# A hand-written order of the tensor engine's side work: joining lone transposes to other small work in the first attention

## The chip, the cores and the metric

One core of one Trainium2 chip runs the whole kernel. The metric is the time of one execution on the device, in microseconds (us). The engines are PE (TensorE, matrix products and transposes, with PEld for its weight loads), ACT (ScalarE), DVE (VectorE), POOL (GpSimd) and SP (SyncE, which issues most DMAs). Each works through a queue of its own in order; they wait for each other on semaphores.

## The reference

A trunk of two layers on `x` of 512 tokens by 1024. The change lies in layer 0, a differential attention with six heads, in parallel with a four-head cross-attention into 256 memory tokens:

```
proj = rms_norm(x) @ w_in_diff            # q, k, v of 6 heads, and the memory's queries
q, k = rms_norm(q) * d**-0.5, rms_norm(k) # per head and map, d = 64, two maps a head
logits = q @ k.T + bias                   # blocks of 128 queries, only the keys of past blocks
p = softmax(logits)                       # per map
w = p[map 0] - lam * p[map 1]
o = rms_norm(w @ v)
x = x + concat(o, memory attention) @ w_out
x = x + conv_ffn(rms_norm(x))
```

Layer 1 has a gated linear attention in place of the differential one; it and the two feed-forward parts are not touched.

## The kernel before, in words

The large products are computed in three terms from operands split into a high and a low part (`whi`, `wlo` for weights, `xsh`, `xsl` for activations), lines 328 to 330 in `gemm`. Weights come by DMA into `raw`, ACT casts them to `whi` (L251) and DVE subtracts for `wlo` (L254). The products of the first attention (`qk` of head pairs 1 and 2, values, the memory's keys and values, the memory's queries) lie in a queue `F` of small pieces, each with an estimated cost, in `ORDER`.

Around these products PE has small work to do for heads whose inputs are ready. Its order is written out by hand in `SCRIPT`: a number lets `F` put out products of about so many microseconds, a letter with a number is one step. PE's instructions stand exactly in that order; those of ACT and DVE are put in order by the framework, which starts from the same program order and may move a later instruction ahead. The steps that matter here:

- `P h`, `prepare`: turns (transposes) the normed `qs` and `ks` of head `h`, four 128x128 blocks each, into a PSUM bank, and ACT copies them to `qT` and `kT` (L696). Heads 2p and 2p+1 share the `qs`, `ks` of pair p.
- `L t`, `M t`, `logits`: the logits of step t (L733) into two banks, `lg` or `tp`; then DVE adds the bias and takes the maximum (L740), ACT takes the exponential (L743), and DVE joins the two maps (L748, L749, L752). There are 15 such steps, five for each pair.
- `T t`, `turn`: transposes the weights of step t into a `tp` bank; ACT copies them to `xt` (L762).
- `V t`, `values`: multiplies them by the values (L774) into an `sm` bank; where a head is complete, `output` follows (Squares, L785). `s h` scales it, `F h` (`finish`) turns it and splits it into high and low (L308, L309).
- `N i`, `norms`: `group_norm` of `qs` or `ks` of a pair, with no work for PE: Squares on ACT (L384), sums on DVE (L385), the reciprocal root on both (L232 to L240), and the multiplication in place on DVE (L390). N4 and N5 are `qs` and `ks` of pair 2, which `P4` and `P5` turn.
- `a`, `b`: operands from the memory tokens. `token_rsqrt` transposes sums of squares of the tokens and makes their reciprocal roots `r_mem`, by which the memory's products are scaled as they leave PSUM.

PSUM has eight banks, two for each of the tags `mm`, `sm`, `lg` and `tp`; a step that asks for a bank waits until the reader of the one before has done.

Of the kernel before, what the change touches and what calls it, by code (L numbers as in the profile page):

```python
# [36 lines left out]
VNAMES = ('v0', 'v0', 'v2')  # L37

SCRIPT = """
    17.75 P0 3.9  # L40
    L0 M1 a3 3.4 P1 5.05 a0 0.97
    1.94 a1 T0
    L2 M3 a2 3.57
    T1 4.86 N2 V0 T2 N3 V1 12.33
    L4 P2 4.55 P3 1.62 V2 T3 2.27 T4
    L5 M6 s0 V3 b1 2.6 V4 1.3 T5 1.3
    L7 M8 3.5 T6 F0 3.64 b0
    V5 T7 8.42 V6 s1 N5 N4 F1
    L9 V7 P4 b2 4.45 T8 T9 s2 3.0
    L10 V8 3.55 X P5 q0  # L50
    L11 b3 V9 T10 4.2
    L12 F2 V10 s3 T11 3.8 q1 k0
# [126 lines left out]
def trunk(ctx, tc, head_d, x_t, mem_t, wpack, cols_a_d, cols_d, conv_d, gate_d, rel_bias, diff_lambda, consts, onehot, out):  # L179
# [12 lines left out]
    def bank(tag):  # L192
        return ps.tile([128, 512], F32, name=f"ps_{tag}", tag=tag)

    def xtile():
        return xs.tile([128, S], F32, name="xt", tag="xs", bufs=XS)

    def split_tiles(pool=None, tag="xs", bufs=XS):
        pool = pool or xs
        return (pool.tile([128, S], F32R, name=tag + "h", tag=tag, bufs=bufs),  # L200
                pool.tile([128, S], F32R, name=tag + "l", tag=tag, bufs=bufs))

    def small(name, bufs=None):
        return cp.tile([128, 16], F32, name=name, tag=name, bufs=bufs)

    def blk(b, w=128):
        return slice(w * b, w * b + w)
# [8 lines left out]
    def transpose(dst, src):  # L216
        n = src.shape[0]
        nc.tensor.transpose(dst, src, ident[:n, :n])  # L218
# [10 lines left out]
    def rsqrt(src, n, inv, on_dve=False, y=None, later=False):  # L229
        v, t = small("rs_v")[:, :n], small("rs_t")[:, :n]  # L230
        y = small("rs_y")[:, :n] if y is None else y
        V.tensor_scalar(v, src, inv, EPS, op0=ALU.mult, op1=ALU.add)  # L232
        if on_dve:
            V.tensor_scalar(t.bitcast(I32), v.bitcast(I32), 1, None, op0=ALU.logical_shift_right)
            V.tensor_scalar(y.bitcast(I32), t.bitcast(I32), -1.0, 1597463007.0, op0=ALU.mult, op1=ALU.add)
            newton(v, y, t)
            newton(v, y, t)
        else:
            A.activation(y, src, AF.Ln, scale=inv, bias=eps)
            A.activation(y, y, AF.Exp, scale=-0.5)  # L240
        if later:
            return y, lambda: newton(v, y, t)
        newton(v, y, t)
        return y
# [48 lines left out]
    def weights(key, by_block=False):  # L293
        i = used[0]
        assert plan[i][0] == key, (plan[i][0], key)
        limit = first_of[i] + WB if by_block else first_of[min(i + 2, len(plan))]
        while done[0] < min(max(limit, first_of[i + 1]), len(order)):
            make_block()
        used[0] += 1
        parts, made[i] = made[i], None  # L300
        return parts

    def freed(i, k):
        if k in [sum(len(b[2]) for b in blocks[i][:j + 1]) - 1 for j in range(len(blocks[i]))] and done[0] < len(order):
            make_block()

    def split(hi, lo, src, gain):
        A.activation(hi, src, AF.Copy, scale=gain)  # L308
        V.scalar_tensor_tensor(lo, src, gain, hi.bitcast(F32), op0=ALU.mult, op1=ALU.subtract)  # L309
# [5 lines left out]
    def gemm(sh, sl, nb, key, w, evac, hook=None, late=False, spare=False):  # L315
        got, open_ = [], {}

        piece = [q[0] for q in plan].index(key)

        def unit(b, k0, k1):  # L320
            if not got:
                got.extend(weights(key, True))
            if k0 == 0:
                open_[b] = bank("tp" if spare and b == 0 else "lg" if late and b > 1 else "mm")[:, :w]
            p = open_[b]
            for k in range(k0, k1):
                hi, lo = got[k]
                mm(p, sh[k][:, blk(b)], hi, start=k == 0, stop=False)  # L328
                mm(p, sh[k][:, blk(b)], lo, start=False, stop=False)  # L329
                mm(p, sl[k][:, blk(b)], hi, start=False, stop=k == KT - 1)  # L330
                if b == nb - 1:
                    freed(piece, k)
            if k1 == KT:
                if hook is not None and b == 0:
                    hook()
                evac(b, open_.pop(b))
        units = [(b, k) for b in range(nb) for k in range(0, KT, 2)]
        if late:
            units.sort(key=lambda u: u[0] == nb - 1 or u[1] == KT - 2)
        for b, k in units:  # L340
            F.add(6 * w / 2370.0, lambda b=b, k=k: unit(b, k, k + 2))
# [23 lines left out]
    r_mem = perm.tile([128, 2], F32, name="r_mem")  # L365

    def col(i, t=cols):
        return t[:, i:i + 1]
# [4 lines left out]
    c_dq, c_dk = col(16), col(17)  # L373
# [52 lines left out]
    def token_rsqrt(tag, sq, nb, y, on_dve=False):  # L426
        p, ss = bank(tag), small("ss")[:, :nb]
        for b in range(nb):
            transpose(p[:, blk(b)], sq[:, blk(b)])
        V.reduce_sum(ss, p[:, :128 * nb].rearrange("p (b n) -> p b n", b=nb), axis=AX.X)  # L430
        return rsqrt(ss, nb, 1.0 / D, on_dve, y=y)
# [11 lines left out]
    with tc.tile_pool(name="ini", bufs=1) as ip, tc.manual_schedule(engines={E.Activation, E.DVE, E.Pool, E.SP}):  # L443
# [8 lines left out]
        p = bank("tp")  # L452
# [48 lines left out]
        for k in range(KT):  # L501
# [24 lines left out]
            for b, i, t in todo:  # L526
                xp, w = terms[i]
# [11 lines left out]
    mem_acc = [None]  # L539

    def mem_squares():
        for i in range(4):
            squares(memT[i], mem_acc)
        sq = mem_acc[0]
        V.tensor_add(sq[:, 0:256], sq[:, 0:256], sq[:, 256:512])


    def mem_kv(l):
        hs, ls = [None] * KT, [None] * KT
        km = [None]  # L550

        def operands(ks=range(KT)):
            if l == 0 and km[0] is None:
                mem_squares()
            if km[0] is None:
                km[0] = xtile().rearrange("p (b n) -> p b n", b=2)
            for k in ks:
                if k % 2 == 0:
                    mh, ml = split_tiles()
                c = blk(k % 2, 256)  # L560
                hs[k], ls[k] = mh[:, c], ml[:, c]
                split(hs[k], ls[k], memT[k // 2][:, c], c_mem(l, k))

        def ev(b, p):
            A.activation(km[0][:, b], p[:, :256], AF.Copy, scale=r_mem[:, b:b + 1])
            A.activation(vm[l][:, b], p[:, 256:], AF.Copy, scale=r_mem[:, b:b + 1])

        def keys(tag="lg"):
            F.need(f"kv{l}")
            p = bank(tag)  # L570
            for hp in range(2):
                for b in range(2):
                    transpose(p[:, 256 * hp + 128 * b:256 * hp + 128 * b + 128], km[0][:, b, blk(hp)])
            A.activation(kmT[l].rearrange("p a b -> p (a b)"), p, AF.Copy, scale=c_mk(l))
        gemm(hs, ls, 2, ("kv", l), 512, ev,
             (lambda: token_rsqrt("lg", mem_acc[0], 2, r_mem)) if l == 0 else None)
        F.add(0.0, lambda: group_norm(None, km[0], 2, 4, 64))
        F.mark(f"kv{l}")
        return operands, keys
# [79 lines left out]
    def diff_layer(pool, mix, acc):  # L659
# [8 lines left out]
        qk = {}  # L668

        def halves(d0, d1):  # L670
            def ev(b, p):
                A.activation(d0[:, b], p[:, :256], AF.Copy, scale=r[:, b:b + 1])
                A.activation(d1[:, b], p[:, 256:], AF.Copy, scale=r[:, b:b + 1])
            return ev
# [13 lines left out]
        def prepare(h):  # L688
            pr, j = divmod(h, 2)
            t2 = []  # L690
            for src, g, nm in zip(qk[pr], (c_dq, c_dk), ("qT", "kT")):
                dst = pool.tile([128, S], F32, name=nm, bufs=3)
                p = bank("tp")
                for b in range(NB):
                    transpose(p[:, blk(b)], src[:, b, blk(j)])
                A.activation(dst, p, AF.Copy, scale=g)  # L696
                t2.append(dst)
            if j == 0:
                pairs[pr] = dict(s2=small("smd").rearrange("p (m b) -> p m b", b=8), nm=small("nmd"), rc=small("rcd"))
            heads[h] = dict(q=t2[0], k=t2[1], v=vs[pr], j=j, left=NB)  # L700
# [106 lines left out]
        ev = halves(*qk[0])  # L807
# [4 lines left out]
        ma = MemAttn(pool, 0, qm, mix, False)  # L812
        ops, keys = [None] * 2, [None] * 2
        for key in ORDER:
# [19 lines left out]
            "N": lambda i: norms(i // 2, i % 2), "a": lambda i: ops[0]((2 * i, 2 * i + 1)),  # L834
            "b": lambda i: ops[1]((2 * i, 2 * i + 1)), "k": lambda i: keys[i]("sm"),
            "q": lambda i: ma.queries() if i else (F.need("v2"), ma.norm()),
            "l": lambda i: ma.logits(i), "t": ma.turn, "v": lambda i: ma.values(i, "sm"),
            "s": lambda i: scales.pop(i)(), "X": lambda i: load_x(x_t),
            "O": lambda i: last.append(out_proj(0, mix, 1, acc, 5)), "!": lambda i: F.flush()}
        do(SCRIPT, doing)  # L840
# [226 lines left out]
    def load_x(src):  # L1067
        for k in range(KT):
            xT[k] = xtile()
            nc.sync.dma_start(xT[k], src[k])  # L1070
# [208 lines left out]
```

## Time and profile before

| what | us |
|---|---|
| median of 3 runs | 1164.59 (1164.59 to 1164.97) |
| the profiled execution, its own time | 1164.66 |
| its span, first to last instruction | 1162.9 |
| PE busy | 1158.3 |
| DVE busy | 752.8 |
| ACT busy | 544.9 |

How to read the lines below. A row of a timeline has the start in us from the span's start, the time to the end of the last of the grouped instructions, the engine, the line of the kernel, the operation, output<-inputs, shapes, and how many; in brackets the idle time of the engine before it and what ended that. Matmuls overlap: one starts before the one ahead has ended, so their cost is read from start to start. A row of the view of waits has who waited, for whom, us in total, how many times, and the longest. `ps_tp` is a bank of tag `tp`, and so on; `C` holds the identity by which PE transposes.

### The profile page before, as it was taken

The numbers are of one execution on the slowest core, as the hardware profiler recorded it, in microseconds if no ns is written. First come the engines' busy times: TensorE is split into PE (matmuls) and PEld (weight loads), VectorE is DVE, ScalarE is ACT, GpSimd is POOL, SyncE is SP. The second block draws the span as 40 slices with busy tenths as digits, with TensorE's granted clock in tenths as the row PEclk, the third lists the DMA queues.
The fourth block names the chain that finished last, engine by engine and source line by source line (L and its number), as shares of the span: only waits on it lengthen the run. The fifth ranks groups of instructions, "written<-read, shape, count | busy, mean of one in ns | idle before, by whom it ended". The sixth has DMA issues, their size and how long they took to land.

```text
span 1162.9 us, 14782 instructions
## 1 busy us (share of the span) xinstructions
PE 1158.3 (100%) x5648; PEld 965.8 (83%) x5648; DVE 752.8 (65%) x1261; ACT 544.9 (47%) x951; POOL 6.5 (1%) x30
## 2 busy tenths in 40 slices
PE   9999999999999999999999999999999999999998
PEld 7888887888888888888888888988888888888887
DVE  7676778688677326677457637867976733576741
ACT  6677686555344213344337634436544421344420
POOL 0000000000000000000000000000000000000000
PEclk9999999999999999999999999999999999999999
DMA  8522242233223223222342220332332323232231
GB/s 285 175 82 83 78 144 70 73 108 128 73 93 125 87 82 121 73 99 94 121 145 68 93 98 11 121 110 101 107 111 73 108 92 109 90 110 73 91 100 45
DMA packets 39652, 117.70 MB, mean 101 GB/s; under 512 B 4767, under 2 KB 7256, under 8 KB 39582
## 3 DMA queue, kind: packets, MB, share of 16 engines
q1 hardware_dynamic: 39150, 116.37, 29.5%
q8 instruction: 44, 0.72, 0.3%
q10 hardware_dynamic: 432, 0.39, 0.1%
q14 instruction: 26, 0.21, 0.1%
HBM read 112.54 MB, written 4.21 MB: 100 GB/s over the span
## 4 chain that ended last, share of the span: by engine, by line
PE 99%; DMA 0%; ACT 0%; DVE 0%; DVEq 0%; issue 0%
PE ps_mm L349 9%; PE ps_mm L350 9%; PE ps_mm L351 9%; PE ps_sm L351 8%; PE ps_sm L349 8%; PE ps_sm L350 8%; PE ps_mm L328 6%; PE ps_mm L330 6%; PE ps_mm L329 6%; PE ps_lg L349 3%; PE ps_tp L351 3%; PE ps_tp L349 3%; PE ps_lg L351 3%; PE ps_lg L350 3%; PE ps_tp L350 3%; PE ps_tp L218 3%
## 5 line engine op out<-in xcount | busy, mean ns | idle before, releaser
L251 ACT CAST whi<-raw 128x1024 fp32r<-128x1024 f32 (+4 forms) x212 | 207.8, 986 | 255.9 <-PE ps_tp L350 120.9
L254 DVE TENSOR_TENSOR wlo<-raw,whi 128x1024 fp32r<-128x1024 f32 (+4 forms) x212 | 240.5, 1139 | 116.3 <-ACT whi L251 115.5
L349 PE MATMUL ps_mm<-xsh,whi 128*128 128x512 f32 x438 | 171.6, 392 | 0.0
L350 PE MATMUL ps_mm<-xsl,whi 128*128 128x512 f32 x438 | 170.6, 389 | 0.0
L351 PE MATMUL ps_mm<-xsh,wlo 128*128 128x512 f32 x438 | 170.5, 389 | 0.0
L349 PE MATMUL ps_sm<-xsh,whi 128*128 128x512 f32 x378 | 147.0, 389 | 0.0
L350 PE MATMUL ps_sm<-xsl,whi 128*128 128x512 f32 x378 | 147.0, 389 | 0.0
L351 PE MATMUL ps_sm<-xsh,wlo 128*128 128x512 f32 x378 | 147.0, 389 | 0.0
L328 PE MATMUL ps_mm<-whi,xsh 128*128 128x512 f32 (+2 forms) x328 | 126.6, 386 | 0.0
L1127 ACT ACTIVATE cvo<-u,cv 128x512 f32<-128x512 f32 x88 | 71.4, 815 | 112.1 <-DVE u L1125 112.1
L330 PE MATMUL ps_mm<-whi,xsl 128*128 128x512 f32 (+2 forms) x328 | 123.0, 375 | 0.0
L329 PE MATMUL ps_mm<-wlo,xsh 128*128 128x512 f32 (+2 forms) x328 | 122.8, 374 | 0.0
L351 PEld LDWEIGHTS ps_mm<-xsh,wlo 128*128 128x128 f32 x438 | 82.2, 188 | 17.2
L350 PEld LDWEIGHTS ps_mm<-xsl,whi 128*128 128x128 f32 x438 | 82.3, 188 | 17.1 <-DVE xsl L309 0.4
L349 PEld LDWEIGHTS ps_mm<-xsh,whi 128*128 128x128 f32 x438 | 82.2, 188 | 17.0 <-issue 0.3
L1128 DVE SCALAR_TENSOR_TENSOR cvo<-u,cv,cvo 128x512 f32<-128x512 f32 x88 | 65.7, 748 | 36.2 <-ACT cvo L1127 36.0
L350 PEld LDWEIGHTS ps_sm<-xsl,whi 128*128 128x128 f32 x378 | 70.9, 188 | 14.7
L351 PEld LDWEIGHTS ps_sm<-xsh,wlo 128*128 128x128 f32 x378 | 70.9, 188 | 14.7
L349 PEld LDWEIGHTS ps_sm<-xsh,whi 128*128 128x128 f32 x378 | 70.9, 188 | 14.7
L330 PEld LDWEIGHTS ps_mm<-whi,xsl 128*128 128x128 f32 x328 | 61.7, 188 | 11.4
L328 PEld LDWEIGHTS ps_mm<-whi,xsh 128*128 128x128 f32 x328 | 61.7, 188 | 11.1 <-issue 0.7
L329 PEld LDWEIGHTS ps_mm<-wlo,xsh 128*128 128x128 f32 x328 | 61.8, 188 | 10.0
(309 smaller groups left out, 1777.7 us busy)
## 6 DMA issues: line engine op xcount, KB each, us to landing
raw<-in_wpack_dram SPq DMA_DIRECT2D x178, 512.0 KB, 3.4
xt<-in_x_t_dram SPq DMA_DIRECT2D x15, 256.0 KB, 5.6
raw<-in_wpack_dram SPq DMA_DIRECT2D x15, 256.0 KB, 5.5
raw<-in_wpack_dram SPq DMA_DIRECT2D x8, 384.0 KB, 3.6
xres<-xt SPq DMA_DIRECT2D x8, 256.0 KB, 3.0
xt<-xres SPq DMA_DIRECT2D x8, 256.0 KB, 5.2
out_dram<-xt SPq DMA_DIRECT2D x7, 256.0 KB, 2.0
bt<-bias_d SPq DMA_DIRECT2D x6, 256.0 KB, 4.7
```

Of the source, the lines that this page charges most:

```text
L218: nc.tensor.transpose(dst, src, ident[:n, :n])
L251: ins = A.copy(hi[:, c], raw[:, c])
L254: V.tensor_sub(lo[:, c], raw[:, c], hi[:, c].bitcast(F32))
L328: mm(p, sh[k][:, blk(b)], hi, start=k == 0, stop=False)
L329: mm(p, sh[k][:, blk(b)], lo, start=False, stop=False)
L330: mm(p, sl[k][:, blk(b)], hi, start=False, stop=k == KT - 1)
L349: mm(p, hi[:, blk(n)], bh, start=i == first, stop=False)
L350: mm(p, hi[:, blk(n)], bl, start=False, stop=False)
L351: mm(p, lo[:, blk(n)], bh, start=False, stop=i == last)
L1127: A.activation(c, u[:, 2:], AF.Identity, scale=cv[l][:, 2, j:j + 1], bias=cv[l][:, 3, j:j + 1])
L1128: V.scalar_tensor_tensor(c, u[:, 1:S + 1], cv[l][:, 1, j:j + 1], c, op0=ALU.mult, op1=ALU.add)
```

## The change

In the script, turns that stood between two runs of products are moved next to other small steps: P1 directly behind P0; T1 behind V0, and V1 behind T2; P3 ahead of L4, with P2 behind it; T5 behind V4; T6 and F0 directly ahead of V5, T7; T8 ahead of V6; T9 ahead of L10. The numbers around them are joined, so that about the same products come out between the steps. P1 turns into the two `sm` banks in place of `tp`. The two transposes of the memory tokens' sums, which hung as a hook on a piece of the memory's products, become a step `w` behind V1. The number of instructions for PE stays the same; what is computed does not change. Two lines fewer stand in the kernel, so its later lines have numbers smaller by one or two.

```diff
 SCRIPT = """
-    17.75 P0 3.9
-    L0 M1 a3 3.4 P1 5.05 a0 0.97
+    17.75 P0 P1 3.9
+    L0 M1 a3 8.45 a0 0.97
     1.94 a1 T0
-    L2 M3 a2 3.57
-    T1 4.86 N2 V0 T2 N3 V1 12.33
-    L4 P2 4.55 P3 1.62 V2 T3 2.27 T4
-    L5 M6 s0 V3 b1 2.6 V4 1.3 T5 1.3
-    L7 M8 3.5 T6 F0 3.64 b0
-    V5 T7 8.42 V6 s1 N5 N4 F1
-    L9 V7 P4 b2 4.45 T8 T9 s2 3.0
+    L2 M3 a2 8.43 N2 V0 T1 N3 2.6 T2 V1 w 9.73
+    P3 L4 P2 6.17 V2 T3 2.27 T4
+    L5 M6 s0 V3 b1 2.6 V4 T5 2.6
+    L7 M8 7.14 T6 F0 b0
+    V5 T7 8.42 T8 V6 s1 N5 N4 F1
+    L9 V7 P4 b2 4.45 s2 3.0 T9
     L10 V8 3.55 X P5 q0
...
-        gemm(hs, ls, 2, ("kv", l), 512, ev,
-             (lambda: token_rsqrt("lg", mem_acc[0], 2, r_mem)) if l == 0 else None)
+        gemm(hs, ls, 2, ("kv", l), 512, ev)
...
-            for src, g, nm in zip(qk[pr], (c_dq, c_dk), ("qT", "kT")):
+            for src, g, nm, tag in zip(qk[pr], (c_dq, c_dk), ("qT", "kT"), {1: ('sm', 'sm')}.get(h, ("tp", "tp"))):
                 dst = pool.tile([128, S], F32, name=nm, bufs=3)
-                p = bank("tp")
+                p = bank(tag)
...
+            "w": lambda i: token_rsqrt("lg", mem_acc[0], 2, r_mem),
```

More of the change, by code (lines that the diff above doesn't have):

```diff
@@ L836, in diff_layer @@
             "q": lambda i: ma.queries() if i else (F.need("v2"), ma.norm()),
-            "l": lambda i: ma.logits(i), "t": ma.turn, "v": lambda i: ma.values(i, "sm"),
+            "w": lambda i: token_rsqrt("lg", mem_acc[0], 2, r_mem), "l": lambda i: ma.logits(i), "t": ma.turn, "v": lambda i: ma.values(i, "sm"),
             "s": lambda i: scales.pop(i)(), "X": lambda i: load_x(x_t),
```

## The prediction

> **What bounds the kernel now.** First the page: engines, chain, clock.
>
> ```profile
> span 1162.9 us, 14782 instructions
> PE 1158.3 (100%) x5648; PEld 965.8 (83%) x5648; DVE 752.8 (65%) x1261; ACT 544.9 (47%) x951; POOL 6.5 (1%) x30
> PEclk9999999999999999999999999999999999999999
> PE 99%; DMA 0%; ACT 0%; DVE 0%; DVEq 0%; issue 0%
> ```
>
> TensorE (PE) is busy all the span and makes 99% of the chain that ended last. Then the view of waits, for PE alone, in whole:
>
> ```profile
> PE ps_tp L454 <- PEq L1234: 0.8, 1, 0.8
> PE ps_mm L528 <- ACT xsh L308: 0.2, 1, 0.2
> ```
>
> After 5 us PE waits for nobody. So there are two ways to move the end: fewer nanoseconds of PE work, or a wait that PE does not have now. A new wait goes into the end in full, since no idle time stands behind it to swallow it. ACT and DVE have room on average, but they run their queues in order: what matters is where a short instruction stands in them, not how busy they are.
>
> **What the change moves.** The built programs hold the same 5333 PE instructions, and SP's and POOL's stand in the same order, so no DMA (weights, bias) moves past another one. PE's order changes inside the first attention only, and ACT's and DVE's with it. I call a run of turns, values and logits between two runs of products an island. Between 47 and 160 us six islands go: P1 joins P0, the two turns of the memory norm join V1 (step w), T1 joins V0, P3 joins L4 P2, T5 joins V4, and T6 F0 join V5 T7 while T8 goes ahead of V6 and T9 ahead of L10.
>
> **Term 1: six islands fewer, a gain.** The timeline of PE around T7 (42 products follow it, to 140.00):
>
> ```profile
> 130.22 0.60 PE L218 MATMUL ps_tp<-C,xt 128*128 128x128 f32 x4
> 130.57 0.48 PE L328 MATMUL ps_mm<-whi,xsh 128*128 128x512 f32 x1
> 130.89 0.40 PE L329 MATMUL ps_mm<-wlo,xsh 128*128 128x512 f32 x1
> 131.12 0.40 PE L330 MATMUL ps_mm<-whi,xsl 128*128 128x512 f32 x1
> ...
> 138.41 0.39 PE L329 MATMUL ps_mm<-wlo,xsh 128*128 128x512 f32 x1
> ...
> 140.00 0.39 PE L330 MATMUL ps_mm<-whi,xsl 128*128 128x512 f32 x1
> 140.23 1.05 PE L774 MATMUL ps_sm<-vv,xt 128*128 128x128 f32 x8
> 141.12 0.60 PE L218 MATMUL ps_tp<-C,o 128*128 128x128 f32 x4
> 141.65 1.13 PE L733 MATMUL ps_lg<-kT,qT 64*128 64x256 f32 x8
> 142.71 1.16 PE L774 MATMUL ps_sm<-vv,xt 128*128 128x128 f32 x8
> 143.71 0.60 PE L218 MATMUL ps_tp<-C,qs 128*128 128x128 f32 x4
> 144.14 0.60 PE L218 MATMUL ps_tp<-C,ks 128*128 128x128 f32 x4
> ```
>
> Starts tell the cost, since the durations overlap. A settled product takes (140.00 - 138.41) / 7 = 0.227. After the turn at 130.22 the next product starts 0.35 later, and the 41 steps from 130.57 to 140.00 take 9.43 instead of 41 x 0.227 = 9.31. A turn that stands alone therefore costs 0.35 + 0.12 = 0.47; one with another turn behind it costs 143.71 to 144.14 = 0.43. Joining an island saves 0.04 to 0.05 and no more: 6 x 0.05 = 0.3. Ends: nothing (a turn's own work is the same anywhere) and twice as much, 0.6.
>
> **Term 2: T8 ahead of V6 holds up the norms of pair 2, a loss.** P4's first four transposes (143.71) need `qs` of pair 2 after its norm, steps N5 N4: Squares on ACT (L384), sums and reciprocal roots, and a multiplication on DVE (L390). The timelines of ACT and DVE show when that is done now:
>
> ```profile
> 130.34 0.47 ACT L673 ACTIVATE ks<-ps_mm,r_x 128x256 f32<-128x256 f32 x1
> ...
> 131.50 0.58 ACT L762 COPY xt<-ps_tp 128x512 f32<-128x512 f32 x1
> 131.96 1.17 ACT L384 ACTIVATE xt<-ks 128x512 f32<-128x512 f32 x2
> ...
> 141.75 0.69 ACT L308 ACTIVATE xsh<-ps_tp,cols 128x512 fp32r<-128x512 f32 x1 [1.85 <-PE ps_tp L218]
> ```
>
> ```profile
> 134.51 0.68 DVE L385 TENSOR_REDUCE ss<-xt 128x8 f32<-128x512 f32 x1
> ...
> 135.93 1.23 DVE L390 TENSOR_TENSOR ks<-ks,rs_y 128x1024 f32<-128x1024 f32 x1
> ...
> 137.49 1.23 DVE L390 TENSOR_TENSOR qs<-qs,rs_y 128x1024 f32<-128x1024 f32 x1
> 142.48 0.75 DVE L309 SCALAR_TENSOR_TENSOR xsl<-ps_tp,cols,xsh 128x512 fp32r<-128x512 f32 x1 [3.77 <-ACT xsh L308]
> 143.14 0.68 DVE L740 CUSTOM_DVE_ANT_0 xt<-ps_lg,bt 128x512 f32<-128x512 f32 x1
> ...
> 143.75 0.69 DVE L740 CUSTOM_DVE_ANT_0 xt<-ps_lg,bt 128x512 f32<-128x512 f32 x1
> ```
>
> The four Squares start at 131.96, right behind T7's copy (L762), and the multiplied `qs` is there at 137.49 + 1.23 = 138.72: a chain of 6.76, done 5.0 before P4. In the changed build the script has T8 ahead of N5 N4, and ACT's queue has T8's copy directly ahead of the four Squares (before, T8 came after P4):
>
> ```
> L760 TensorCopy xt_1506<-ps_tp_1501      (T8's copy)
> L383 Activation xt_1519<-ks_459 ... xt_1539<-qs_458   (the four Squares)
> ```
>
> So the Squares can't start before PE has turned T8, behind the 42 products. In the times of before (earlier terms shift everything alike):
>
> - T8 starts where V6 stands, 140.23, and is turned at 140.23 + 0.60 = 140.83. F1's rows (141.12 + 0.60, ACT at 141.75) give 0.03 until ACT starts, so the copy is at 140.86, and the Squares 131.96 - 131.50 = 0.46 later, at 141.32. That is 9.4 later than now.
> - The chain of 6.76 ends at 148.08 if nothing else stands in its queues. But it now runs when F1 and L9 do, and in the built order DVE has F1's low half (142.48 to 143.14, 0.66) and L9's two bias sums (0.61 each, 143.14 to 143.75) ahead of the `qs` multiplication: 1.88 together. Part of it falls into the hole of the chain where DVE waits for ACT's Ln and Exp, 134.51 + 0.68 = 135.19 to 135.93, 0.74. At least 1.88 - 0.74 = 1.1 is added; at most 1.88 and F1's 0.69 on ACT, which stands between a Ln and its Exp, 2.6. I take 1.4, near the lower end, because the low half is about as long as the hole. `qs` is ready at 149.5.
> - PE asks for it at 143.71 plus T8's 0.43 = 144.14.
>
> The wait is 149.48 - 144.14 = 5.3, with ends 5.1 and 6.5. Queued behind it on PE are P4, the rest of the products and thus everything; all of it moves. Nothing is late next: during the wait ACT, DVE and the weights' DMAs run ahead.
>
> A stall of that length may cost more than itself. The timeline of PE at the start:
>
> ```profile
> 0.77 3.32 PE L454 MATMUL ps_tp<-const-float32-0.0 128*128 128x512 f32 x6 [0.77 <-PEq L1234]
> 4.29 1.33 PE L528 MATMUL ps_mm<-whi,xsh 128*128 128x256 f32 x4 [0.20 <-ACT xsh L308]
> 5.43 1.05 PE L528 MATMUL ps_sm<-whi,xsh 128*128 128x512 f32 x2
> 6.28 0.66 PE L528 MATMUL ps_mm<-wlo,xsh 128*128 128x512 f32 x2
> 6.77 0.62 PE L528 MATMUL ps_sm<-wlo,xsh 128*128 128x512 f32 x2
> 7.23 0.62 PE L528 MATMUL ps_mm<-whi,xsl 128*128 128x512 f32 x2
> ```
>
> Two products take 0.85 at 5.43 and 0.46 from 6.77: PE runs at about half speed until 6.3, 5.5 after its first matmul, though the page's PEclk shows full tenths there. No row shows what an idle PE does later, since it never is. [...] In the sum I leave it at nothing and make it a rival, priced from the rows.
>
> **Term 3: banks asked for sooner, a small loss.** The turning banks (`tp`) are two. Where islands merge, a turn asks for a bank that ACT has not yet emptied. Rows of ACT:
>
> ```profile
> 31.75 0.52 ACT L673 ACTIVATE ks<-ps_sm,r_x 128x256 f32<-128x256 f32 x1
> ...
> 94.19 1.05 ACT L251 CAST whi<-raw 128x1024 fp32r<-128x1024 f32 x1 [0.52 <-DMA raw<-in_wpack_dram]
> 95.48 0.21 ACT L240 ACTIVATE rs_y<-rs_y 128x8 f32<-128x8 f32 x1
> 98.14 0.67 ACT L696 ACTIVATE qT<-ps_tp,cols 128x512 f32<-128x512 f32 x1
> 126.10 1.99 ACT L251 CAST whi<-raw 128x1024 fp32r<-128x1024 f32 x2
> ```
>
> P3 L4 P2: P2 asks about 2.0 after P3 starts (two turns of 0.43, logits of 1.06 as 141.65 to 142.71). P3's first copy can start when ACT is through its weights and roots (95.69) and takes 0.67: free at about 96.4, asked for at 94.9 + 2.0. It fits, unless the weights' cast, which waits for a DMA, is 0.5 later: then 0.3 for each bank. T6 F0 V5 T7: T7 asks for T6's bank 1.75 after T6 (0.43, 0.43, 0.89); ACT has a cast of 1.0, two evacuations and the copy of 0.58 to do in that time: 0 to 0.5. I take 0.2 at each place, 0.4 together, ends 0 and 1.1.
>
> P1's early turns take the `sm` banks, emptied by 31.75 + 0.52, long before P0 and P1: nothing. Covers: its two copies on ACT delay a weight cast by 1.3, hidden by two pieces of weights in hand; without that, up to 1.3. Step w makes the memory's roots in another place, still ahead of the first evacuation that scales by them: nothing.
>
> **Sum.** The profiled execution took 1164.66 (span 1162.9, and 1.8 around it), 0.07 over the median of 1164.59. 5.3 + 0.4 - 0.3 = +5.4: 1170.1 us. Own range 1169.2 (5.1 + 0 - 0.6) to 1172.3 (6.5 + 1.1).
>
> **Rivals.**
>
> - *The clock falls in the stall.* PE comes back at half speed. Price from the start: a slow stretch of 2.0 (4.29 to 6.28) to 5.5 us, of which 0.47 is lost (0.43 against 0.23 for a product), 0.9 to 2.6; middle 1.7. Time: 1171.8. For it: the slow start. [...]
> - *The stall is not there: not slower.* If the four Squares ran ahead of T8's copy, as ACT has them before, the chain ends at 138.7, 5 us ahead of P4, and what is left is +0.4 - 0.3: 1164.7. It turns on one place, whether L384 on `ks` starts before T8 is turned. `ks` itself is evacuated by 130.34 + 0.47 = 130.81, so data allows it; the order of ACT's queue speaks against it.
> - *The change does not do what it says.* Turns side by side cost 0.43 and alone 0.47: with no gain at all the sum is 0.3 higher, 1170.4, within the range. Alone it decides nothing.
>
> **How the numbers follow.** Forecast 0.53, clock 0.43, no stall 0.03, the rest 0.01. The range takes the forecast's own low end rounded, 1169.0, and up to 1173.0, which holds the clock's middle with the upper half of its price; outside lie the early Squares and the longest slow stretches. A measurement of this kernel can tell 0.2%, 2.3 us: slower than 1166.9 are the forecast and the clock, 0.96; within 0.2% 0.03; faster 0.01.
>
> **What would show it.** In the profile after: a wait of 5 to 6 us of PE for DVE `qs` at P4, near 144 to 150 us, the first entry of PE's waits; the Squares on `ks` at about 141, behind T8's copy; no other wait of PE over 0.5. PE's busy time, the wait left out, falls by 0.3. If the clock fell, products behind P4 start 0.43 apart for some us. Wrong would be: Squares at 132, a wait under 3 us, or a PE time that grows elsewhere.

## The result and the profile after

| kernel | median us | lowest to highest | ratio to before, 95% interval |
|---|---|---|---|
| before | 1164.59 | 1163.94 to 1164.97 (5 runs) | |
| after | 1172.66 | 1171.74 to 1175.09 (5 runs) | 1.0072 [1.0061, 1.0084] |

The changed kernel is 0.7% slower, 8.1 us. The forecast was 1170.1, its range ended at 1173.0. The median lies inside, 2.6 above the forecast, one of the five runs (1175.09) lies outside, and the case that happened is the rival in which the clock falls.

The profiled execution of after took 1172.66 itself. From its page, the same lines that were shown of before, with the row of slices of the granted clock:

```profile
span 1170.9 us, 14783 instructions
PE 1160.8 (99%) x5648; PEld 967.6 (83%) x5648; DVE 751.6 (64%) x1261; ACT 545.7 (47%) x951; POOL 6.5 (1%) x30
PEclk9999989999999999999999999999999999999999
PE 95%; ACT 2%; DVE 1%; DMA 1%; issue 0%; DVEq 0%; ACTq 0%
```

The span grew by 8.0. PE's busy time grew by 2.5, although it has the same 5648 instructions, and where the prediction had a fall of 0.3: something ran slower. The chain that ended last now goes through ACT and DVE for 3% of the span, and in the sixth slice, 146 to 176 us, the digit of the clock is an 8. The view of waits, PE alone, in whole:

```profile
PE ps_tp L217 <- DVE rcd L746: 5.2, 1, 5.2
PE ps_tp L453 <- PEq L1232: 0.8, 1, 0.8
PE ps_tp L217 <- ACT qT L694: 0.2, 1, 0.2
```

There is one new wait of 5.2 us (the 0.2 for `qT` is P2's, at 96.60). The view names the DVE instruction that it takes for the releaser, a small one right behind; what P4's transposes read is `qs`, whose multiplication (L389) ends at nearly the same moment, 149.36 against 149.43. The timelines of PE, ACT and DVE of after, around the place:

```profile
139.94 0.40 PE L329 MATMUL ps_mm<-whi,xsl 128*128 128x512 f32 x1
140.17 0.60 PE L217 MATMUL ps_tp<-C,xt 128*128 128x128 f32 x4
...
149.51 1.08 PE L217 MATMUL ps_tp<-C,qs 128*128 128x128 f32 x4 [5.25 <-DVE rcd L746]
...
151.67 0.63 PE L328 MATMUL ps_mm<-wlo,xsh 128*128 128x512 f32 x1
152.10 0.63 PE L329 MATMUL ps_mm<-whi,xsl 128*128 128x512 f32 x1
...
155.08 0.40 PE L327 MATMUL ps_mm<-whi,xsh 128*128 128x512 f32 x1
155.32 0.40 PE L328 MATMUL ps_mm<-wlo,xsh 128*128 128x512 f32 x1
```

```profile
140.81 0.59 ACT L760 COPY xt<-ps_tp 128x512 f32<-128x512 f32 x1 [0.96 <-PE ps_tp L217]
141.30 1.15 ACT L383 ACTIVATE xt<-ks 128x512 f32<-128x512 f32 x2
```

```profile
147.33 0.68 DVE L738 CUSTOM_DVE_ANT_0 xt<-ps_lg,bt 128x512 f32<-128x512 f32 x1
148.14 1.22 DVE L389 TENSOR_TENSOR qs<-qs,rs_y 128x1024 f32<-128x1024 f32 x1
```

Read in this order: T8's turn (140.17), its copy on ACT (140.81), the Squares behind it (141.30), one of L9's bias sums on DVE, ahead of the multiplication (147.33), the multiplied `qs` (148.14 + 1.22 = 149.36), P4 (149.51). Behind P4 the products start 0.43 apart (151.67 to 152.10), and only from 155.08 on 0.24. The view of stretches shows the granted clock there; its columns are the stretch, its length, PE's busy time and instructions, the granted clock, and the DMAs' share and rate:

```profile
148.20:148.24 0.04, 0.00 (x0) 1.00 0.00 0
148.26:148.30 0.04, 0.00 (x0) 0.50 0.00 0
155.08:155.12 0.04, 0.04 (x2) 1.00 0.00 0
148.25:151.66 3.41, 2.15 (x9) 0.50 0.23 77
151.66:155.07 3.41, 3.41 (x9) 0.50 0.00 0
```

The clock was halved at 148.25, while PE waited, and came back by 155.08: 6.83 us, in 2.15 + 3.41 = 5.56 of which PE had work. In the 3.41 us ahead of the fall, 144.84 to 148.25, PE did nothing at all.

The profile shows one execution. Half speed for 6.83 us makes a mean granted clock of 1 - 0.5 x 6.83 / 1171 = 0.997. Four of the five executions of after have this mean on record; the fifth, 1171.74, has 0.999, so it spent at most about 3.5 us at half speed. The length of the slow stretch is not the same every time.

**Where the 8 us came from**, by starts on PE. P0 starts at 46.72 here, at 47.11 in before; the last product starts at 1166.88 here, at 1158.88 in before:

```profile
46.72 0.60 PE L217 MATMUL ps_tp<-C,qs 128*128 128x128 f32 x4
...
1166.88 0.39 PE L350 MATMUL ps_tp<-midh,wlo 128*128 128x512 f32 x1
```

```profile
47.11 0.60 PE L218 MATMUL ps_tp<-C,qs 128*128 128x128 f32 x4
...
1158.88 0.39 PE L351 MATMUL ps_tp<-midh,wlo 128*128 128x512 f32 x1
```

- P0 to the last product ahead of T8: 139.94 - 46.72 = 93.22, where before had 140.00 - 47.11 = 92.89: the joins cost 0.33.
- The wait: 5.25.
- P4 to the end: 1166.88 - 149.51 = 1017.37. Before had 1158.88 - 143.71 = 1015.17 with T8's turn of 0.43 inside, so 1014.74: 2.63 more, by the clock.
- Sum 8.21. P0 itself came 0.39 sooner in this execution; the remainder to the 8.00 at the last product, 0.18, lies between T8 and P4. Nearly all of it comes from the way the wait is counted: idle time begins at the end of the values, 143.10 + 1.16, while P4 would have started 1.00 after their start (142.71 to 143.71 in before), 0.16 sooner. By starts the wait is 5.41.

### The profile page after: what moved, and what is told of

Its sections match the earlier page's. It is cut to its first block, busy times and chain, and to the rows that moved or that the text cites. A ratio compares the mean times of both kernels' runs of the same rounds, so it can differ in the third digit from the quotient of the medians.

```text
span 1170.9 us, 14783 instructions
## 1 busy us (share of the span) xinstructions
PE 1160.8 (99%) x5648; PEld 967.6 (83%) x5648; DVE 751.6 (64%) x1261; ACT 545.7 (47%) x951; POOL 6.5 (1%) x30
## 4 chain that ended last, share of the span: by engine, by line
PE 95%; ACT 2%; DVE 1%; DMA 1%; issue 0%; DVEq 0%; ACTq 0%
PE ps_mm L348 9%; PE ps_mm L350 9%; PE ps_mm L349 9%; PE ps_sm L348 7%; PE ps_sm L350 7%; PE ps_sm L349 7%; PE ps_mm L327 5%; PE ps_mm L329 5%; PE ps_mm L328 5%; PE ps_tp L350 3%; PE ps_lg L350 3%; PE ps_tp L348 3%; PE ps_lg L348 3%; PE ps_lg L349 3%; PE ps_tp L349 3%; PE ps_tp L217 3%
```

## The experiments

The lines changed are those of the script; after has `V5 T7 8.42 T8 V6 s1 N5 N4 F1` and, below it, `L9 V7 P4 b2 4.45 s2 3.0 T9`.

**1. T8 and T9 back, all other moves kept** (after as the base):

```diff
-    V5 T7 8.42 T8 V6 s1 N5 N4 F1
-    L9 V7 P4 b2 4.45 s2 3.0 T9
+    V5 T7 8.42 V6 s1 N5 N4 F1
+    L9 V7 P4 b2 4.45 T8 T9 s2 3.0
```

> The changed kernel with T8 back behind P4, next to T9, as it was before; the five other joins stay. Theory (T8's copy holds up the norms of pair 2, and the clock falls in the wait that follows): the wait of 5.2 us at P4 and the slow stretch both go, the clock stays 1.000, and what is left are the other joins: 1164.4 us, 0.2 less than before, at most 0.5 apart from it. Rival (the joins themselves, the memory's roots in step w, or banks asked for sooner cost the time): the time stays near 1172.

Measured: 1164.69 (1164.26 to 1165.88), ratio 1.0003 [0.9995, 1.0012], granted clock 1.000. Its view of waits has no entry for P4, and its timeline of PE around the joins is:

```profile
46.60 0.60 PE L217 MATMUL ps_tp<-C,qs 128*128 128x128 f32 x4
...
139.80 0.39 PE L329 MATMUL ps_mm<-whi,xsl 128*128 128x512 f32 x1
```

139.80 - 46.60 = 93.20, again 0.31 more than before. The whole loss beyond that goes with T8.

**2. T8 alone moved, nothing else** (before as the base):

```diff
-    V5 T7 8.42 V6 s1 N5 N4 F1
-    L9 V7 P4 b2 4.45 T8 T9 s2 3.0
+    V5 T7 8.42 T8 V6 s1 N5 N4 F1
+    L9 V7 P4 b2 4.45 T9 s2 3.0
```

> The kernel before with one edit alone: T8 ahead of V6, T9 where it was. Theory: the whole loss is here, a wait of 5.2 to 5.4 us of TensorE at P4 on the norm of qs, and a fall of the clock that costs up to 2.6 us more: 1170 to 1173 us, as in the changed kernel. Rival (the joins share the loss): well under 1170.

Measured: 1171.96 (1171.46 to 1173.03), 1.0068 [1.0055, 1.0081]. P4 in its timeline of PE:

```profile
149.90 1.09 PE L218 MATMUL ps_tp<-C,qs 128*128 128x128 f32 x4 [5.25 <-DVE rcd L748]
```

One step moved makes the wait and the slow clock (slow from 148.56 to 155.39, 6.83 again). The two experiments together show that T8's place is sufficient and, in this kernel, necessary.

**3. T8 stays ahead of V6, the norms go ahead of the products** (after as the base). This tells the queue of ACT from the place of T8 as such:

```diff
-    V5 T7 8.42 T8 V6 s1 N5 N4 F1
+    V5 T7 N5 N4 8.42 T8 V6 s1 F1
```

> The changed kernel with T8 still ahead of V6, but with N5 N4 ahead of the products that come before T8, so that the Squares stand in front of T8's copy in ScalarE's queue. Theory (the order of copy and Squares in the queue): Squares at about 132 us, no wait at P4, clock 1.000, 1164.3 us. Rival (T8's place on TensorE, or what VectorE does for F1 and L9 at that time, holds P4 up): a wait of 1 to 5 us at P4 stays.

Measured: 1165.07 (1164.48 to 1167.21), 1.001 [1.0002, 1.0019]. ACT has the Squares behind T7's copy, as in before, and P4 does not wait (the only entry of 0.2 in its view of waits is P2's, at 99.04):

```profile
133.74 0.58 ACT L760 COPY xt<-ps_tp 128x512 f32<-128x512 f32 x1
134.21 1.17 ACT L383 ACTIVATE xt<-ks 128x512 f32<-128x512 f32 x2
```

T8 can stay where the change put it; what costs is that the Squares stand behind a copy that comes so late. The 0.8 over the expectation is mostly the joins, counted at -0.3 there and measured at +0.3 (49.15 to 142.33 on PE, 93.18). The profiled execution was the longest one, 1167.21: its first products ran at half speed until about 10 us, which is told at the end.

**4 and 5. PE kept busy in the wait.** A step `D` between V7 and P4 runs 22 products that nobody reads, into an `lg` bank (4) or a `tp` bank (5):

```diff
-    L9 V7 P4 b2 4.45 s2 3.0 T9
+    L9 V7 D P4 b2 4.45 s2 3.0 T9
...
+        def keep_busy():
+            p = bank("lg")      # kept_busy_tp: bank("tp")
+            for i in range(22):
+                mm(p, xh[i % KT][:, blk(0)], xh[(i + 1) % KT], start=True, stop=True)
...
```

> The changed kernel with 22 more products (128x512, some 5.0 us) that nobody reads between V7 and P4: they fill the wait and do no work of the result. Theory (the 2.6 us beyond the wait come from the clock, which falls because TensorE idles): the wait shrinks to 0.2 to 0.6 us, the clock stays 1.000, products behind P4 start 0.23 apart, and the time is 1169.6 to 1170.2 us, 2.5 under the changed kernel. Rival (TensorE is slow behind the wait because weights, copies or banks have to start again): products behind P4 start later than 0.23 apart as before, and the time stays near 1172.6.

Measured: 1171.88 (1171.57 to 1172.07), 1.0065 [1.0051, 1.0079]; the expectation was missed by 1.7. The timeline of PE shows that the filler spoilt the experiment:

```profile
146.28 5.30 PE L833 MATMUL ps_lg<-xsh 128*128 128x512 f32 x22 [1.98 <-DVE nmd L738]
151.42 0.60 PE L217 MATMUL ps_tp<-C,qs 128*128 128x128 f32 x4
```

It waited 1.98 for DVE to read L9's logits out of the bank, and P4 came at 151.42, 1.9 later than in after. 1170.1 + 1.9 is what was measured. So it was run again with the other bank:

> As kept_busy, but the 22 products that nobody reads go into a tp bank, which is empty by then, in place of a lg bank, which VectorE still read for L9: there the filler itself waited 2.0 us and left TensorE 1.9 us later than needed. Theory (the 2.6 us beyond the wait come from the clock, which falls because TensorE idles): filler from 144.1 to 149.1, a wait of 0.2 to 0.6 us at P4, clock 1.000, products behind P4 0.23 apart, 1169.8 to 1170.4 us. Rival (starting again behind a wait costs it): near 1172.6 us.

Measured: 1170.7 (1169.82 to 1172.32), 1.0049 [1.0037, 1.0062]. The median is 0.3 over what the clock theory expected, and 2.0 under after. The profiled execution took 1169.82, its granted clock was 1.000, and PE goes straight through:

```profile
143.72 5.27 PE L833 MATMUL ps_tp<-xsh 128*128 128x512 f32 x22
149.22 0.63 PE L217 MATMUL ps_tp<-C,qs 128*128 128x128 f32 x4 [0.23 <-DVE rcd L746]
...
150.35 0.39 PE L328 MATMUL ps_mm<-wlo,xsh 128*128 128x512 f32 x1
150.58 0.40 PE L329 MATMUL ps_mm<-whi,xsl 128*128 128x512 f32 x1
...
1163.91 0.39 PE L350 MATMUL ps_tp<-midh,wlo 128*128 128x512 f32 x1
```

From P4 to the last product, the same instructions as in after: 1163.91 - 149.22 = 1014.69, against 1017.37. With P4 at nearly the same moment, the slow clock alone is worth 2.68 in these two executions; the medians differ by 2.0.

**6. A shorter wait.** 2.12 us of products moved behind T8:

```diff
-    V5 T7 8.42 T8 V6 s1 N5 N4 F1
+    V5 T7 6.3 T8 2.12 V6 s1 N5 N4 F1
```

> The changed kernel with T8 2.1 us of products sooner, in an island of its own ahead of V6: T8's copy, the Squares and the end of the norm come 2.1 us sooner, and TensorE asks for qs when it did. Theory: a wait of 3.1 to 3.4 us at P4. [...] If the wait did not come from T8's copy, it stays 5.2 us and the time near 1172.

Measured: 1170.32 (1169.84 to 1171.37), 1.0043 [1.003, 1.0057]. The wait shrank to 3.27, so 1164.7 + 3.3 = 1168.0 is what it would give with a full clock. The profiled execution took 1171.37, and its timeline of PE and its stretches show the clock falling all the same:

```profile
148.10 1.09 PE L217 MATMUL ps_tp<-C,qs 128*128 128x128 f32 x4 [3.27 <-DVE rcd L746]
```

```profile
146.72:146.76 0.04, 0.00 (x0) 0.50 0.00 0
153.56:153.60 0.04, 0.04 (x1) 1.00 0.00 0
143.29:146.70 3.41, 1.54 (x14) 1.00 0.01 2
```

It fell at 146.70, when PE had stood still for 146.70 - (148.10 - 3.27) = 1.87 us: in the 3.41 us before, PE was busy for 1.54, 45%. It was back 6.8 us later, by 153.56. From P4 to the last product it took 1165.60 - 148.10 = 1017.50, 2.8 more than in kept_busy_tp. The other four runs, 1.8 to 2.4 above 1168.0, have no trace. Their mean granted clock is 0.998 in one and 0.999 in three, against 0.997 in the profiled one, so they spent less time at half speed. No run without a wait has 0.998. Some have 0.999, as the profiled execution of keep_gains below, whose clock is 0.50 only behind the last product, from 1161.2 on; so in those three a shorter fall is likely, not shown.

**7. Are the joins worth anything?** After with P3, T6 F0, T8 and T9 where before has them, the other joins kept:

```diff
-    P3 L4 P2 6.17 V2 T3 2.27 T4
+    L4 P2 4.55 P3 1.62 V2 T3 2.27 T4
...
-    L7 M8 7.14 T6 F0 b0
-    V5 T7 8.42 T8 V6 s1 N5 N4 F1
-    L9 V7 P4 b2 4.45 s2 3.0 T9
+    L7 M8 3.5 T6 F0 3.64 b0
+    V5 T7 8.42 V6 s1 N5 N4 F1
+    L9 V7 P4 b2 4.45 T8 T9 s2 3.0
```

> The changed kernel with those joins undone that brought a wait: P3, T6 with F0, and T8 with T9 stand as before; P1 with P0, T1 with V0, step w and T5 with V4 stay. Four islands fewer than before, no new wait. From the first small turns to the last product the trace should be 0.1 to 0.2 us shorter than that of the kernel before, by the saving seen up to 93 us in the changed kernel (0.12); the time 1164.3 us, which the runs can't tell from before. If joins cost more than they save, it is longer than before by 0.1 or more.

Measured: 1164.49 (1164.21 to 1164.99), 0.9995 [0.9986, 1.0004]. The timeline of PE:

```profile
46.86 0.60 PE L217 MATMUL ps_tp<-C,qs 128*128 128x128 f32 x4
...
139.62 0.39 PE L329 MATMUL ps_mm<-whi,xsl 128*128 128x512 f32 x1
```

92.76 against 92.89: 0.13. In this stretch the trace has 13 islands where before has 16 (and after 11): three fewer, not the four that were expected, since T1 in joining V0 splits T2 and V1 off. That is 0.04 each, seen in the starts of one execution and too small for the times. It is the best version found, and not measurably better than before.

**8 and 9. How long may PE wait?** Experiment 5 with fewer products in the filler:

```diff
-            for i in range(22):
+            for i in range(16):     # filler_11: range(11)
```

> As kept_busy_tp with 16 in place of 22 products that nobody reads: TensorE works until about 147.7 us and then waits some 1.6 us at P4 for the norm, which is ready at the same time as before. [...]

> The same with 11 such products: a wait of some 2.7 us at P4. [...]

Waits of PE, first with 16, then with 11:

```profile
PE ps_tp L217 <- DVE rcd L746: 1.6, 1, 1.6
```

```profile
PE ps_tp L217 <- DVE rcd L746: 2.7, 1, 2.7
```

With 16: 1170.51 (1169.77 to 1170.68), 1.0044 [1.0031, 1.0057]; clock 1.000 in the trace, no time that asks for a fall. With 11: 1171.18 (1170.1 to 1173.71), 1.0055 [1.0041, 1.0068]; the profiled execution, 1170.12, kept its clock at 1.000, the slowest is 3.6 above the fastest. The mean granted clock is 0.999 in the three longer runs and 1.000 in the two others, which would fit a short fall; but 0.999 occurs without a wait too, and kept_busy_tp spreads by 2.5 without need of a fall. That falls happened with 11 is inferred, not shown.

**10. T8 still ahead of V6, but early enough.** After with the turn behind 5.5 us of products in place of 8.42:

```diff
-    V5 T7 8.42 T8 V6 s1 N5 N4 F1
+    V5 T7 5.5 T8 2.92 V6 s1 N5 N4 F1
```

> The changed kernel with T8 2.9 us of products sooner (0.8 sooner than in short_stall). In ScalarE's queue T8's copy still stands ahead of the Squares, but the last evacuation of values and memory queries, which waits for the products before V6, now stands behind them. Theory (what stands ahead of the Squares in ScalarE's queue, and when TensorE lets it go, sets the wait): Squares at about 138 us, the norm ready before P4, no wait over 0.2 us, clock 1.000, 1164.7 us. Rival (T8 ahead of V6 costs the wait wherever it is): a wait of about 2.4 us.

Measured: 1164.86 (1164.66 to 1165.5), 1.0001 [0.9992, 1.001], clock 1.000. The timelines of ACT and PE:

```profile
136.73 0.59 ACT L760 COPY xt<-ps_tp 128x512 f32<-128x512 f32 x1 [2.32 <-PE ps_tp L217]
137.21 1.16 ACT L383 ACTIVATE xt<-ks 128x512 f32<-128x512 f32 x2
```

```profile
144.14 0.60 PE L217 MATMUL ps_tp<-C,qs 128*128 128x128 f32 x4
```

The copy still stands ahead of the Squares, and ACT still waits for it, 2.32. But the chain from the Squares on now ends at 143.93, and P4 asks at 144.14. Nothing is left of the loss. The gain is more than T8's own shift: its copy comes 1.88 sooner than in experiment 6 (138.61 there), but `qs` is ready 4.03 sooner (147.96 there). The chain from the Squares on takes 6.72, as in before, where experiment 6 took 8.87, because the last evacuation on ACT now comes behind the Squares and not among them, and the work of F1 and L9 on DVE behind the multiplication.

## Why the prediction was right, and where it was not

**Term 2, the wait, was right step by step.** Predicted: Squares at 141.32, `qs` ready at 149.48, a wait of 5.3 by starts. Measured: 141.30, 149.36, 5.41 by starts, 5.25 of idle time. The chain took 8.06 in place of 6.76, so what DVE and ACT put into it added 1.3, where 1.4 was taken. Experiments 1, 2, 3 and 10 show the reason too: with T8 back, with the norms ahead, or with T8 early, the wait is gone.

**Term 3 was right in place and small in size.** P2 waits for its banks in P3 L4 P2, and T7 for its bank in T6 F0 V5 T7. The timeline of PE in after:

```profile
95.30 1.13 PE L731 MATMUL ps_lg<-kT,qT 64*128 64x256 f32 x8
96.60 0.66 PE L217 MATMUL ps_tp<-C,qs 128*128 128x128 f32 x4 [0.17 <-ACT qT L694]
97.18 0.66 PE L217 MATMUL ps_tp<-C,ks 128*128 128x128 f32 x4
...
128.96 1.06 PE L772 MATMUL ps_sm<-vv,xt 128*128 128x128 f32 x8
130.12 0.66 PE L217 MATMUL ps_tp<-C,xt 128*128 128x128 f32 x4
```

96.60 - 95.30 = 1.30 where logits in a quiet place take 1.06, and 0.58 from the first turn to the second where it is 0.43: 0.39. 130.12 - 128.96 = 1.16 where values took 0.89 before: 0.27. Together 0.66, where 0.4 was taken of 0 to 1.1.

**Term 1 holds in direction.** Up to T8 the net of all joins is +0.33 and their waits are 0.66, so the five islands that went there saved 0.33, where the prediction had 0.3 for six (the sixth, T8 T9, stood behind P4); three of them saved 0.13 in experiment 7. That is 0.04 to 0.07 for each, predicted 0.04 to 0.05. The two small terms did not cancel to +0.1 as in the sum, but to +0.33.

**The step that failed is the clock, set to nothing in the sum.** The prediction gave the fall 0.43 and the forecast without it 0.53. No run shows where these two come from: behind the first 5 us PE waits for nobody in before, so they were the author's estimate. What the runs showed is a fall in all three traced executions with a wait of 3.27 or 5.25 (experiment 6, experiment 2 and after). Judged by them, with a wait of 5.3 the fall was the likely case, and the sum should have held it. The forecast's own high end was 1172.3; the measured 1172.66 lies inside only because the range was drawn on to 1173.0 for the rival. The sign that belonged to the forecast, PE's busy time 0.3 less, was wrong: it grew by 2.5.

**Its price was mis-sized as well.** The rival took 0.9 to 2.6, middle 1.7, from the slow start; measured are 2.63 and 2.68, a little past the upper end. The middle stood for a slow stretch halfway between 2.0 and 5.5 us of work. In the traces it lasts 6.83 us, of which in after the first 1.26 fall into the wait: 5.56 us of half speed lose 2.8 by halves, 2.6 to 2.7 by starts. The sum with the measured clock is 1164.66 + 5.3 + 0.4 - 0.3 + 2.7 = 1172.8, and the profiled execution took 1172.66.

**The rival without a stall** would have been 1164.7, and the three kernels with T8 behind P4 (experiment 1), the norms first (3) or T8 early (10), in which the Squares come in time, give 1164.69 to 1165.07. The price was right; the order of ACT's queue decided against the case, as argued.

## What to carry to other kernels

A move that is free on the bound engine can cost on an engine that is half idle: look at what its short follow-up (here a copy) is put ahead of in that engine's queue, and date the follow-up by the engine that releases it. When a wait on the bound engine is costed, add what the clock does after it; here a wait of 3.3 us was followed by 2.8 us of lost speed in the traced execution, and filling a wait with products that nobody reads kept the clock at 1.000 in the traced execution (experiment 5, 2.68 us less from P4 to the last product than in after). If a step has to go ahead of a chain, move it far enough ahead: 2.9 us of products made the difference between 8 us and none.

## What the runs showed of the hardware

- The granted clock was 0.50 for 6.83 us in all three executions whose rows show a fall (after, T8 alone, the shorter wait). In after, PE was busy for 2.15 of the first 3.41 us of that stretch and throughout the second 3.41, and behind it the clock was 1.00 again. (The rows of both stand in the view of stretches above.) The mean clocks of the runs without a trace (0.998 in one run of the shorter wait and 0.999 in one of after, against 0.997 in the profiled executions of both) speak for shorter slow stretches.
- The fall came when PE had stood still for 148.25 - (149.51 - 5.25) = 3.99 us in after, 148.56 - (149.90 - 5.25) = 3.91 with T8 alone, and 1.87 with the shorter wait. With 11 products of filler PE stood still for 2.7, and the clock stayed at 1.000 in the profiled execution. So the time that PE stands still does not tell by itself whether the clock falls.
- Nor does the share of work. In the 3.41 us before the fall PE was busy for 0.00 in after and with T8 alone, and for 45% with the shorter wait. With 16 products of filler, 3.41 us with nearly all of the wait of 1.6 in them show a full clock:

```profile
147.65:151.06 3.41, 1.83 (x12) 1.00 0.27 77
```

  PE was busy for 1.83, 54%, and the clock stayed. With 11, a stretch as long that holds the whole wait of 2.7 has 3.41 - 2.7 = 0.7 of work in it, 21% (an estimate from the length of the wait), and there too the clock stayed. What decides on a fall, no run shows.
- The slow speed at the kernel's start ends at different moments in different executions: by 5.36 us in after (the two products from there take 5.83 - 5.36 = 0.47), at 6.3 in before, and at some 10 in the profiled one of experiment 3, whose timeline of PE has products 0.43 apart at 8.56 and 0.23 apart only from 10.13:

```profile
8.56 1.05 PE L527 MATMUL ps_mm<-whi,xsl 128*128 128x512 f32 x2
9.41 0.88 PE L527 MATMUL ps_sm<-whi,xsl 128*128 128x512 f32 x2
10.13 0.40 PE L527 MATMUL ps_mm<-whi,xsh 128*128 128x512 f32 x1
10.36 0.40 PE L527 MATMUL ps_mm<-wlo,xsh 128*128 128x512 f32 x1
```

P0 then stood at 49.15 in place of 47.11. That moves the whole execution by 2 us, as much as the cost of a fall, so a difference of this size needs the starts within one trace, and not only the times.
